# A hybrid decoder layer on one core: the order of instructions and the places of tiles drawn again, with activation functions of one table kept together

## The chip, the cores and the metric

The kernel runs on one core of a Trainium2 chip. The metric is the device time of one execution in microseconds. The kernel before was timed in three runs: 811.6, 809.67 and 811.94 us, with a median of 811.6 us.

## What is computed

One layer of a decoder over 512 tokens of width 1024, in float32: three token mixers side by side, each with a gate, then a projection, and a SwiGLU feed-forward network, with RMS norms ahead of and behind both.

```python
u = rms_norm(h, ln_mix_pre[l])
proj = jnp.einsum('bsd,de->bse', u, w_in[l])
qa, ka, va, qb, kb, vb, qm, gl = jnp.split(proj, split_idx, axis=-1)
y_swa = swa_sink_attention(...)          # window 128, 8 query heads
y_sb = stick_breaking_attention(...)     # 8 heads, log_sigmoid and exp
y_mem = memory_cross_attention(...)      # 4 heads, softmax over 256 memory rows
g = jax.nn.sigmoid(gl.reshape(B, S, N_BRANCH, D))
merged = g[:, :, 0] * (y_swa @ w_swa) + g[:, :, 1] * (y_sb @ w_sb) + g[:, :, 2] * (y_mem @ w_mem)
mix = jnp.einsum('bse,ed->bsd', merged, w_out[l])
h = h + rms_norm(mix, ln_mix_post[l])
u = rms_norm(h, ln_ffn_pre[l])
a = jax.nn.silu(jnp.einsum('bsd,df->bsf', u, w_gate[l])) * jnp.einsum('bsd,df->bsf', u, w_up[l])
ffn = jnp.einsum('bsf,fd->bsd', a, w_down[l])
h = h + rms_norm(ffn, ln_ffn_post[l])
```

So ScalarE needs sigmoid for the gates and the stick-breaking heads, Exp for both softmaxes, Ln and Exp for every inverse root of a norm, and silu's table set in the FFN.

## The kernel before

Every fp32 product is done as three matmuls: a tile is split into a high part (`hi`, a cast on ScalarE) and a remainder (`lo`, a subtraction on VectorE), and hi·hi, hi·lo and lo·hi are added up in PSUM (`mm3`). The big projections and the FFN are cut into two by two blocks, with seven products in place of eight. Sums of weight blocks come out of DMAs that add while they load (`raw` and `wide` tiles), others from VectorE.

The stages are: the first norm and projections (to about 80 us), the stick-breaking heads (80 to 205), the sliding-window heads in four pairs (`swa_pair`, from 205), gates and branch projections, the memory attention in two pairs (`mem_pair`, 318 to 363, tiles `mw`, `mpts`), the memory gates and the sum of the three branches (`merge`, tiles `mg`), the mixing (about 420 to 480), the FFN (480 to 793) and the last norm.

In the mixing, `mix(t)` does one block t of 128 tokens. Eight times three matmuls for each half fill two PSUM banks. ScalarE squares both with a sum (`mt<-p`), `rstd_small` makes the inverse root from the sums with a Ln and an Exp on ScalarE and four small steps on VectorE (tiles `s`), VectorE scales the bank (`mt<-p,s,bc_g_post`), and adds it to the residual (`xr`). A second square, a second Ln and Exp, and a scaling (`mt<-xr,s,bc_g_fpre`) make the FFN's input, which TensorE transposes (`turn(t)`, `p<-c_ident,mt`). ScalarE casts it out of PSUM into the FFN's right-hand sides (`B11h`, `B21h`, `T1h` and so on). The first gate of the FFN is a sigmoid `sg` and a product `aq` on VectorE. At the end `dn_half` does the same kind of norm for the output: `sqr`, Ln, Exp, and `fg`.

PSUM has eight banks, `p0` to `p7`. `raw`, `hi`, `lo` have four places each, small tiles (`s`) sixteen and tiles of 128x512 (`ck`) 73. Class `Places` hands them out: the n-th tile of a kind goes to the place that the table `PLAN` gives.

The order on each engine is fixed. `tile_kernel` first issues all instructions, stage by stage, and class `Noted` writes down each (its inner function is line 186, which is why the profile has this line for all). The last loop adds, for each engine, a chain of order-only dependencies by the table `ORDER`, whose ranges are indices of the recorded instructions. `table(name)` records an explicit load of a set of activation functions; there are nine of these. The build then puts another table load ahead of any activation whose function isn't in the set that is loaded at that point of ScalarE's list.

The lines in question:

```python
nc.scalar.activation(tmp[h][:, :], ps[h][:, :], AF.Square, accum_out=ss[:, h : h + 1])
fn(t, s1, AF.Ln, bias=b, scale=1.0 / D)          # rstd_small
fn(r, t, AF.Exp, scale=-0.5)
table("natural_log_exp_and_others")               # ahead of mix_mm(0, 0, KC)
table("silu_and_others")                          # behind mix(3)
for part in text.split():                         # text is a row of ORDER
    a, _, b = part.partition("-")
    for k in range(int(a), int(b or a) + 1):
        if last is not None:
            follow(seen[k], seen[last])
        last = k
```

Of the kernel before, what the change touches and what calls it, by code (L numbers as in the profile page):

```python
# [100 lines left out]
    ),  # L101
    "gpsimd": (
        "5-8 4 9-12 2-3 0-1 13-14 16 15 17 31-32 18-19 24 29 20-23 25-28 30 33-36 38-39 41 37 42 40 43-50 52 51 54 53 "
        "55-59 61 60 62-66 69 67 72 68 70-71 73-79 81 80 82-89 91 90 92-117 129-132 118-119 133 120-121 134 122-128"
# [1952 lines left out]
```

## Time and profile before

| | us |
|---|---|
| median of three runs | 811.6 (809.67 to 811.94) |
| profiled execution | 809.63, span 807.9 |
| granted TensorE clock, mean | 0.991 |
| idle time of TensorE, start to 80 us | 2.29 |
| DMA from HBM | 125.70 MB, 161 GB/s over the span |

The page's slices show where TensorE is not full, in tenths of each fortieth of the span (20.2 us):

```profile
PE   8999999999999999989998979999999999999994
ACT  7663778976966675798947896445454547758765
PEclk9999999999999999999999999999999999999998
DMA  8543864534599888898998017986777755879302
```

A 9 is 90% or more. TensorE (PE) falls to 8 or 7 in four slices ahead of the last: those that begin at 0, 343, 424 and 465. ScalarE (ACT) is never full for long. The table loads are instructions of ScalarE, named ACT_TABLE_LOAD, and no line of the program's own but of the helper.

### The profile page before, as it was taken

To read this page: it belongs to the slowest core of one execution; us is meant where nothing else is said; L and a number is where in the kernel's file an instruction comes from. 1 tells how busy PE (TensorE), PEld (TensorE's weight loads), DVE (VectorE), ACT (ScalarE), POOL (GpSimd) and SP (SyncE) were. 2 spreads that over 40 slices of the span, in tenths; PEclk is the share of its full clock that TensorE was granted. 3 is DMA by queue.
4 is the path that set the end of the run, shared out by engine and by line. 5 is a ranking of instruction groups with operands and counts; after the bars stand their busy time and mean duration, and the time that the engine had idled before them with its cause. 6 is when DMAs were issued, how large, how long until landed. Compare 5 with 4: busy or idle time off the path is not lost.

```text
span 807.9 us, 12635 instructions
## 1 busy us (share of the span) xinstructions
PE 776.7 (96%) x4686; PEld 680.9 (84%) x4686; DVE 618.3 (77%) x997; ACT 547.2 (68%) x926; POOL 110.0 (14%) x139
## 2 busy tenths in 40 slices
PE   8999999999999999989998979999999999999994
PEld 6899898778689887778786779999999999888883
DVE  7995786678786856878976479877777778998865
ACT  7663778976966675798947896445454547758765
POOL 3110300110112112311021000100000000215000
PEclk9999999999999999999999999999999999999998
DMA  8543864534599888898998017986777755879302
GB/s 289 172 111 117 295 186 132 130 75 107 93 233 183 188 190 182 204 270 193 247 284 157 0 32 188 269 224 179 183 184 187 179 153 184 163 182 198 57 0 104
DMA packets 47565, 135.43 MB, mean 168 GB/s; under 512 B 5520, under 2 KB 7104, under 8 KB 47504
## 3 DMA queue, kind: packets, MB, share of 16 engines
q0 software_dynamic: 16640, 50.61, 34.2%
q1 hardware_dynamic: 30432, 83.63, 31.7%
q8 instruction: 36, 0.59, 0.3%
q10 hardware_dynamic: 432, 0.39, 0.2%
q14 instruction: 25, 0.20, 0.1%
HBM read 125.70 MB, written 4.72 MB: 161 GB/s over the span
## 4 chain that ended last, share of the span: by engine, by line
PE 42%; ACT 6%; DVE 2%; issue 1%; DVEq 0%; ACTq 0%
PE p L186 42%; ACT L186 3%; ACT mt L186 1%; DVE mt L186 1%; ACT s L186 1%; DVE s L186 0%; ACT hi L186 0%; DVE fg L186 0%; DVE xr L186 0%; DVE mg011l L186 0%; ACT sqr L186 0%; DVEq L2045 0%; ACT B11h L186 0%; ACT mg011h L186 0%; ACT mg001h L186 0%
## 5 line engine op out<-in xcount | busy, mean ns | idle before, releaser
L186 DVE TENSOR_TENSOR lo<-raw,hi 128x1024 fp32r<-128x1024 f32 (+5 forms) x118 | 134.0, 1138 | 41.4 <-ACT hi L186 40.6
L186 ACT CAST hi<-raw 128x1024 fp32r<-128x1024 f32 (+5 forms) x118 | 116.2, 986 | 71.8 <-PE p L186 56.4
L186 ACT CAST hi<-wide 128x1024 fp32r<-128x1024 f32 x83 | 87.2, 1052 | 83.9 <-PE p L186 50.2
L186 DVE TENSOR_TENSOR lo<-wide,hi 128x1024 fp32r<-128x1024 f32 x83 | 101.4, 1223 | 39.9 <-ACT hi L186 39.6
L186 ACT ACT_TABLE_LOAD x47 | 60.3, 1283 | 7.0 <-DVE s L186 4.1
L186 PE MATMUL p<-hi,uh 128*128 128x512 f32 (+1 forms) x160 | 58.1, 363 | 2.4 <-ACT mw L186 2.4
L186 PE MATMUL p<-lo,lh 128*128 128x512 f32 x154 | 59.9, 389 | 0.0
L186 PE MATMUL p<-hi,lh 128*128 128x512 f32 x154 | 59.9, 389 | 0.0
L186 PE MATMUL p<-hi,ll 128*128 128x512 f32 x154 | 59.9, 389 | 0.0
L186 PE MATMUL p<-lo,uh 128*128 128x512 f32 (+1 forms) x160 | 57.4, 359 | 0.0
L186 PE MATMUL p<-hi,ul 128*128 128x512 f32 (+1 forms) x160 | 57.2, 358 | 0.0
L186 PE MATMUL p<-uh,hi 128*128 128x512 f32 (+1 forms) x136 | 50.9, 375 | 1.4 <-ACT uh L186 0.9
L186 PE MATMUL p<-uh,lo 128*128 128x512 f32 (+1 forms) x136 | 49.6, 365 | 0.0
L186 PE MATMUL p<-ul,hi 128*128 128x512 f32 (+1 forms) x136 | 49.6, 366 | 0.0
L186 PEld LDWEIGHTS p<-hi,uh 128*128 128x128 f32 x160 | 30.2, 189 | 6.6 <-ACT mw L186 3.1
L186 POOL DMA_DIRECT2D raw<-in_w_gu x17 | 14.6, 861 | 148.5 <-DMA raw<-in_w_gu 148.1
L186 PEld LDWEIGHTS p<-hi,lh 128*128 128x128 f32 x154 | 28.9, 188 | 6.0
L186 PEld LDWEIGHTS p<-hi,ll 128*128 128x128 f32 x154 | 28.9, 188 | 6.0
L186 PEld LDWEIGHTS p<-lo,lh 128*128 128x128 f32 x154 | 28.9, 188 | 5.9
L186 PEld LDWEIGHTS p<-hi,ul 128*128 128x128 f32 x160 | 30.1, 188 | 3.8
L186 PEld LDWEIGHTS p<-lo,uh 128*128 128x128 f32 x160 | 30.2, 189 | 3.4
L186 DVE TENSOR_TENSOR_SCAN bw<-br,bw 128x512 f32<-128x512 f32 (+3 forms) x32 | 23.9, 804 | 10.3 <-ACT bw L186 10.3
(878 smaller groups left out, 2490.1 us busy)
## 6 DMA issues: line engine op xcount, KB each, us to landing
wide<-in_w_gu SPq DMA_DIRECT2D x31, 512.0 KB, 4.8
raw<-in_w_gu SPq DMA_DIRECT2D x26, 512.0 KB, 4.7
raw<-in_w_g POOLq DMA_DIRECT2D x18, 512.0 KB, 5.6
raw<-in_w_gu POOLq DMA_DIRECT2D x17, 512.0 KB, 7.1
raw<-in_w_g SPq DMA_DIRECT2D x14, 512.0 KB, 4.7
raw<-in_w_p SPq DMA_DIRECT2D x11, 512.0 KB, 4.9
bp<-in_w_dn SPq DMA_DIRECT2D x22, 256.0 KB, 4.4
wide<-in_w_gu POOLq DMA_DIRECT2D x10, 512.0 KB, 5.9
```

The costliest lines, as they stand in the source:

```text
L186: ins = f(*args, **kw)
```

## The change

The tables `ORDER` and `PLAN` are replaced by others; no code outside them differs. In `ORDER` the rows of TensorE, VectorE, ScalarE, GpSimd and SyncE are others; in `PLAN` the places of `lo`, `p`, `ck`, `s`, `fraw` and `flo`. Two rows of ScalarE's table, before and now:

```diff
-        "358 354 359 369 356 361-364 370 365-368 371-375 380 376-379 381 394 382-383 408 384-385 414-415 395-396 "
-        "418-419 386-389 397 390-393 402 398-399 409 403 410 400-401 411 424 404-405 425 406-407 412-413 433-434 416 "
+        "361-364 370-372 365-368 373-376 380 377-379 381 394-396 382-385 414-415 418-419 386-389 397 390-393 402 "
+        "398-399 408 403 400-401 409 404-405 410-411 406-407 412-413 424-425 416 433-434 440 417 441 432 449 420-421 "
```

Line numbers shift by two, so that the helper is line 188 in the changed kernel. The counts of all instructions are the same, except for ScalarE's table loads: 47 before and 9 now, the explicit ones. The numbers behind a name stand for its buffer.

ScalarE at the start of the memory attention's exponentials (`mw`), where `hi_76` is a cast of a branch weight. Before:

```order
L186 ACTIVATE gq0p_2992<-p_106,wide_84 128x512
L186 CAST hi_78<-raw_72 128x1024
L186 CAST hi_76<-wide_84 128x1024
L186 ACT_TABLE_LOAD
L186 ACTIVATE mw_3019,s_90<-p_110,s_93,wide_84 128x256 x2
L186 ACTIVATE mw_3020,s_90<-p_111,s_93,wide_84 128x256 x2
```

And now:

```order
L188 ACTIVATE gq0p_2992<-p_109,wide_84 128x512
L188 CAST hi_78<-raw_72 128x1024
L188 ACT_TABLE_LOAD
L188 CAST hi_76<-wide_84 128x1024
L188 ACTIVATE mw_3019,s_90<-p_110,s_88,wide_84 128x256 x2
L188 ACTIVATE mw_3020,s_90<-p_111,s_88,wide_84 128x256 x2
```

The table load has moved ahead of the cast `hi_76`; the exponentials stand behind both as before.

ScalarE in the mixing, with the end of block 0 and the squares, Ln and Exp of block 1: `mt_3999<-p` and `mt_4000<-p` are block 1's two squares, the small activations on `s` are Ln and Exp, first of block 0's second norm and then of block 1's first, and `mt_3999<-xr` is block 1's second square. Before:

```order
L186 ACTIVATE mt_3999,s_90<-p_106 128x512
L186 ACT_TABLE_LOAD
L186 ACTIVATE s_93<-s_91,s_92 128x1
L186 CAST hi_77<-wide_84 128x1024
L186 ACT_TABLE_LOAD
L186 ACTIVATE s_91<-s_93 128x1
L186 ACTIVATE mt_4000,s_90<-p_105 128x512
L186 ACT_TABLE_LOAD
L186 ACTIVATE s_91<-s_90,s_88 128x1
L186 ACT_TABLE_LOAD
L186 ACTIVATE s_89<-s_91 128x1
L186 ACTIVATE mt_3999,s_91<-xr_3814 128x512
```

And now:

```order
L188 ACTIVATE mt_3999,s_88<-p_107 128x512
L188 ACTIVATE s_89<-s_91,s_90 128x1
L188 CAST hi_77<-wide_84 128x1024
L188 ACTIVATE s_90<-s_89 128x1
L188 ACTIVATE mt_4000,s_88<-p_104 128x512
L188 ACTIVATE s_90<-s_88,s_93 128x1
L188 ACTIVATE s_92<-s_90 128x1
L188 ACTIVATE mt_3999,s_90<-xr_3814 128x512
```

The order of squares, cast, Ln and Exp is the same, and the four table loads between them are gone.

VectorE at the end of the mixing: `s` is the last step of block 3's inverse root, `mt_4186` and `mt_4187` are block 3's FFN input, which TensorE waits for, and `aq` the product of the first gate of the FFN. Before:

```order
L186 TENSOR_TENSOR lo_81<-raw_72,hi_76 128x1024
L186 SCALAR_TENSOR_TENSOR s_88<-s_93,s_88 128x1
L186 TENSOR_TENSOR aq_4309<-gp_4259,sg_4307 128x256
L186 SCALAR_TENSOR_TENSOR mt_4186<-xr_3822,s_88,bc_g_fpre_3832 128x512
L186 SCALAR_TENSOR_TENSOR mt_4187<-xr_3823,s_88,bc_g_fpre_3833 128x512
L186 TENSOR_TENSOR N2l_4382<-t_4269,N2h_4381 128x2x128
```

And now:

```order
L188 TENSOR_TENSOR lo_81<-raw_72,hi_76 128x1024
L188 SCALAR_TENSOR_TENSOR s_90<-s_88,s_90 128x1
L188 TENSOR_TENSOR N2l_4382<-t_4269,N2h_4381 128x2x128
L188 SCALAR_TENSOR_TENSOR mt_4186<-xr_3822,s_90,bc_g_fpre_3832 128x512
L188 SCALAR_TENSOR_TENSOR mt_4187<-xr_3823,s_90,bc_g_fpre_3833 128x512
L188 TENSOR_TENSOR aq_4309<-gp_4259,sg_4307 128x256
```

`aq` has moved behind the two `mt`, and the subtraction `N2l` ahead of them.

At the end of the kernel the last rows of ScalarE are the same but for eight table loads that are gone. On SyncE and GpSimd only the order among the FFN's weight loads (`raw<-in_w_gu` and `wide<-in_w_gu`) is another: 46 and 10 rows of difference.

More of the change, by code (lines that the diff above doesn't have):

```diff
@@ L120 @@
     "lo": (
-        "0 1 2 3 1 2 0 3 1 2 0 3 1 2 0 3 1 2 0 3 1 2 0 3 1 2 0 3 1 2 0 3 1 0 2 3 1 0 2 3 1 0 2 3 1 0 2 3 1 0 2 3 1 0 2 "
-        "3 1 0 2 3 1 0 2 3 1 0 2 3 1 0 2 3 1 0 2 3 1 0 2 3 1 0 2 3 1 0 2 3 1 0 2 3 1 0"
+        "0 1 2 3 1 2 0 3 1 2 0 3 1 2 0 3 1 2 0 3 1 2 0 3 1 2 0 3 1 2 0 3 1 2 0 3 1 2 0 3 1 2 0 3 1 2 0 3 1 2 0 3 1 2 0 "
+        "3 1 2 0 3 1 2 0 3 1 2 0 3 1 2 0 3 1 2 0 3 1 2 0 3 1 2 0 3 1 2 0 3 1 2 0 3 1 2"
     ),
     "p": (
[5 rows of a table removed]
[5 rows of a table added]
     ),
@@ L132 @@
         "1 3 4 6 13 15 18 8 10 12 16 17 19 21 23 22 24 25 27 26 29 28 30 14 3 31 32 4 14 14 4 33 34 35 3 31 32 36 37 31 "
[19 rows of a table removed]
[19 rows of a table added]
     ),
     "s": (
-        "0 3 2 1 0 2 0 3 1 2 0 1 0 3 2 1 0 2 0 3 1 2 5 4 5 2 4 5 5 2 4 5 5 3 4 2 3 4 4 1 5 3 2 3 0 5 3 1 1 5 0 1 2 1 3 "
-        "0 1 2 2 3 5 6 0 6 4 5 6 0 0 4 5 0 0 5 3 1 4 10 8 9 6 0 10 4 2 10 4 0 7 4 0 10"
+        "0 3 2 1 0 2 0 3 1 2 0 1 0 3 2 1 0 2 0 3 1 2 0 1 0 2 1 0 0 2 1 0 0 3 1 2 3 0 2 4 1 2 0 2 5 1 2 4 4 0 5 6 1 6 3 "
+        "5 6 1 1 3 0 4 5 4 2 0 4 2 2 5 0 2 2 0 3 1 5 10 8 9 4 2 10 5 6 10 5 2 7 5 2 10"
     ),
     "fraw": (
-        "4 5 0 1 3 2 7 8 6 4 5 0 1 3 4 2 6 1 0 8 4 7 5 3 2 1 8 6 0 4 5 2 3 7 1 6 4 8 0 5 3 1 7 2 6 8 5 4 0 3 7 6 2 1 8 "
-        "4 3 5 0 7 2 8 1"
+        "4 5 0 1 3 2 8 7 6 4 5 0 1 3 4 2 6 1 7 0 8 4 3 5 2 1 0 7 6 8 3 2 5 4 1 7 8 6 0 3 5 1 4 2 7 6 3 0 8 5 4 7 2 1 6 "
+        "0 5 8 3 4 2 6 1"
     ),
```

166 rows, old and new, of tables (ORDER, PLAN) are left out of this document.

## The prediction

> **What bounds the kernel now.** I first read the page's busy list and the page's list of the costliest groups, which say what there is to win:
>
> ```profile
> PE 776.7 (96%) x4686; PEld 680.9 (84%) x4686; DVE 618.3 (77%) x997; ACT 547.2 (68%) x926; POOL 110.0 (14%) x139
> L186 ACT ACT_TABLE_LOAD x47 | 60.3, 1283 | 7.0 <-DVE s L186 4.1
> ```
>
> TensorE is busy for 776.7 us of a span of 807.9, so 31.2 us is all that an order can give back, apart from matmuls that ran at a lower clock. ScalarE spends 60.3 us in 47 table loads of 1283 ns. ScalarE is busy for 68% only, so those 60.3 us are no gain in themselves. A load counts where TensorE, or the end of the kernel, waits for what stands behind it. So the next view is the busy time by stage. Its columns are the stretch, its length, the busy time of PE, PEld, DVE, ACT and POOL (with counts), the granted clock, the share of time that the DMA engines were busy, and GB/s.
>
> ```profile
> 205.00:225.00 20.00, 18.15 (x99) 13.95 (x98) 16.24 (x50) 19.21 (x46) 3.45 (x4) 1.00 0.57 99
> 318.00:331.00 13.00, 10.55 (x44) 8.00 (x43) 10.46 (x23) 10.42 (x24) 1.72 (x2) 0.87 0.70 177
> 331.00:348.00 17.00, 17.00 (x96) 14.73 (x95) 14.81 (x23) 12.93 (x20) 6.10 (x7) 1.00 0.99 220
> 348.00:363.00 15.00, 12.77 (x62) 9.79 (x61) 10.85 (x22) 14.94 (x32) 2.71 (x3) 1.00 1.01 272
> 432.00:449.00 17.00, 13.46 (x57) 10.66 (x55) 7.60 (x19) 12.43 (x23) 0.86 (x1) 0.90 0.55 114
> 449.00:467.00 18.00, 14.44 (x73) 11.38 (x71) 8.69 (x25) 14.88 (x31) 0.00 (x0) 1.00 0.00 0
> 467.00:480.00 13.00, 10.47 (x86) 10.29 (x87) 10.15 (x22) 11.54 (x22) 0.00 (x0) 1.00 0.06 8
> 480.00:793.00 313.00, 313.00 (x2213) 295.50 (x2214) 254.97 (x349) 187.38 (x290) 35.53 (x41) 1.00 0.66 166
> ```
>
> Length less PE's busy time is TensorE's idle time: 1.85 us in the sliding-window attention (205 to 225), 2.45 and 2.23 in the memory attention (318 to 331 and 348 to 363), and 3.54, 3.56 and 2.53 in the mixing (432 to 480), which is 9.63 there. In the FFN (480 to 793) it is zero, whatever ScalarE does. Behind 793 the kernel only finishes. TensorE's list of waits (what it waited for, us in all, times, the longest) names who held it up:
>
> ```profile
> PE p L186 <- DVE mt L186: 7.3, 4, 3.5
> PE p L186 <- ACT mw L186: 3.0, 3, 1.8
> PE p L186 <- ACT B11h L186: 2.3, 1, 2.3
> ```
>
> `mt` and `B11h` are tiles of the mixing, `mw` the weights of the memory attention. All of them are made on ScalarE, or on VectorE right behind ScalarE, just where the loads stand.
>
> **The change, part by part.** The instructions are the same on every engine, except that ScalarE's list has 9 table loads in place of 47. The FFN's weight loads, and many rows on the other engines, change places by a few rows.
>
> *The mixing.* For each block of 128 tokens two squares give sums, Ln and Exp give the inverse root, and VectorE's `mt` empties the PSUM bank that TensorE needs next. ScalarE, VectorE and TensorE show this for block 1:
>
> ```profile
> 435.90 1.28 ACT L186 ACT_TABLE_LOAD   x1 [1.40 <-DVE s L186]
> 437.19 0.29 ACT L186 ACTIVATE s<-s,s 128x1 f32<-128x1 f32 x1
> 437.51 1.28 ACT L186 ACT_TABLE_LOAD   x1
> 438.80 0.20 ACT L186 ACTIVATE s<-s 128x1 f32<-128x1 f32 x1
> 439.49 1.41 DVE L186 SCALAR_TENSOR_TENSOR mt<-p,s,bc_g_post 128x512 f32<-128x512 f32 x2
> 437.02 0.39 PE L186 MATMUL p<-wo07h,mg111l 128*128 128x512 f32 x1
> 440.95 0.50 PE L186 MATMUL p<-wo10h,mg001h 128*128 128x512 f32 x1 [3.54 <-DVE mt L186]
> 442.25 0.63 PE L186 MATMUL p<-wo11l,mg001h 128*128 128x512 f32 x1
> 442.68 0.63 PE L186 MATMUL p<-wo11h,mg001l 128*128 128x512 f32 x1
> 432.43 1.28 ACT L186 ACT_TABLE_LOAD   x1
> ```
>
> From 435.90 to the end of `mt` at 439.49 + 1.41 = 440.90 it is 5.00 us, 2 x 1.28 of it loads; 2.44 is left. The load at 432.43, and the one before its Ln, push back the chain of block 0 ahead of it, so the start moves 2.56 earlier as well, to 433.34, and the bank is free at 435.78. TensorE needs it when its last matmul before the wait (start 437.02) is through, 0.39 later at the latest, so the wait of 3.54 goes, with more than a us to spare. That is why block 1 pays for four loads but gives back no more than the wait. A second loss goes with it: right behind the wait matmuls start 442.68 - 442.25 = 0.43 apart, and the clock of this stretch is 0.90, that is at most 17 x 0.10 = 1.7 us lost; I take 1.5. Blocks 2 and 3 have the same chain. The last wait differs:
>
> ```profile
> 476.93 1.28 ACT L186 ACT_TABLE_LOAD   x1
> 479.91 0.63 PE L186 MATMUL p<-c_ident,mt 128*128 128x128 f32 x4 [2.53 <-DVE mt L186]
> ```
>
> On VectorE `mt` stands behind `aq`, the first gate of the FFN, which needs a sigmoid with its own load (476.93). The new order puts `mt` ahead of `aq`, and this load's place in the chain goes with the two of Ln and Exp: 3.84 against a wait of 2.53. What comes next is the cast `B11h` behind the copies and squares on ScalarE: I leave 0.5 us for it. **Term: 9.63 + 1.5 - 0.5 = 10.6.** From both sides: 11.3 if nothing is left (9.63 + 1.7), and 5.3, half, if casts and copies, which now run one behind the other, take the loads' place.
>
> *The end.* Five rows of the chain that ended last, with a row of ScalarE and one of TensorE at the same time:
>
> ```profile
> 793.93 1.28 ACT L186
> 797.52 1.41 DVE fg L186 x2
> 799.01 1.28 ACT L186
> 800.62 1.28 ACT L186
> 802.15 0.23 DVE s L186
> 796.95 0.58 ACT L186 ACTIVATE sqr<-p 128x512 f32<-128x512 f32 x1
> 796.17 0.39 PE L186 MATMUL p<-hi,ll 128*128 128x512 f32 x1
> ```
>
> From 793.93 to 800.62 four loads stand on this chain, 5.13 us. The first two hold back block 2's last `fg`, and behind that VectorE starts block 3's sums. The other two lie between block 3's sums and its last scale at 802.15. Without them block 2 is out of the way, and block 3 waits for TensorE alone, whose last matmul ends at 796.17 + 0.39 = 796.56. Behind it come the square with its sum (0.7), VectorE's sum (0.1), Ln 0.29, Exp 0.20, by the rows of block 1 above, and VectorE's product with the gain, which was done beside a load and now is 0.7 in the path less what Ln and Exp cover: 1.5 in all, so 798.05 for what starts at 802.15. **Term: 4.1**, between 2.6 (the last two loads alone) and 5.1 (all four).
>
> *The memory attention.*
>
> ```profile
> 320.93 1.05 ACT L186 CAST hi<-wide 128x1024 fp32r<-128x1024 f32 x1 [1.72 <-DMA wide<-in_w_brt]
> 322.00 1.28 ACT L186 ACT_TABLE_LOAD   x1
> 324.55 0.50 PE L186 MATMUL p<-hi,uh 128*128 128x512 f32 x1 [1.78 <-ACT mw L186]
> 221.73 0.50 PE L186 MATMUL p<-hi,xsp60h 128*128 128x512 f32 x1 [1.49 <-ACT hi L186]
> 397.20 1.05 ACT L186 CAST hi<-wide 128x1024 fp32r<-128x1024 f32 x1 [1.08 <-DMA wide<-in_w_brt]
> ```
>
> At 318 to 331 the load for Exp stands behind a cast that waits 1.72 us for its transfer. Now it stands ahead of the cast and hides in this wait, so the exponentials `mw` come 1.3 us sooner, and the bank that they empty is taken up later. Of the idle 2.45, and of 13 x 0.13 = 1.7 lost to the clock (taken as 1.25), I leave 0.7: **3.0**, from 1.3 (the load alone) to 4.15. At 348 to 363 two loads and gate sums around the second pair's exponentials go: 2.6 us sooner against an idle time of 2.23: **2.2**, from 0 (if the transfers set this stretch, whose DMA share is 1.01) to 2.3.
>
> *The smaller ones.* At 205 to 225 two loads stood ahead of the cast for which TensorE waits 1.49 us; the idle time there is 1.85, of which I take **1.3** (0 to 1.85). The cast at 397.20 waits 1.08 us for a transfer, not for a load: **0**, from -1 to 1, since transfers move. In the FFN the loads of table sets, and two at its end, lie where TensorE never waits: **0**. The new order of weight loads in it costs nothing while casts run ahead of TensorE; what it costs otherwise is the last rival's price.
>
> **The sum** is 10.6 + 4.1 + 3.0 + 2.2 + 1.3 = 21.2 us. The profiled execution took 809.63 us (span 807.9 and 1.7 around it), so 788.4. The three runs have their median at 811.6, 2.0 above; the next median may lie as far above its profile, so up to 790.4. I take **788.5**, near the lower end, since every residue has been left out of the gain already.
>
> **Two rules weighed.** The rows above show a load ending at 435.90 + 1.28 = 437.18 and the Ln starting at 437.19. The Trainium skill, "ScalarE: Activation LUTs", section "What ACT_TABLE_LOAD costs", puts a drain of the pipeline on top of the load, about 2.7 us for a switch. By that the four loads of the end would hold 4 x 2.7 = 10.8, an estimate; the trace has no room for it, and the load alone is counted.
>
> The clock fell behind a wait of 3.54 (stretch of 0.90), and with a longest wait of 1.78 (stretch of 0.87), but not behind the wait of 2.53 (1.00). The Trainium skill, "TensorE: Matmul & The Clock Gate", section "Part 1: The HAM clock gate", lets the clock halve after an idle window of about 3.4 us. The first and the last agree, the second does not; by that page its 1.25 would stay out of the sum, which would give 789.8.
>
> **The rivals.**
>
> *Transfers take the place* of the wait. In 331 to 348 and 348 to 363 the DMA engines are busy 0.99 and 1.01 of the time, and two casts wait for transfers already (320.93 and 397.20). If TensorE gets there sooner and the weights don't, the memory attention's 3.0 + 2.2 comes back as a wait for DMA: 788.5 + 5.2 = 793.7. Against it: nothing in the mixing hangs on it, where the share is 0.55 and below. Chance 0.17.
>
> *Half of the mixing stays*, since the squares, copies and casts on ScalarE (12.43 and 14.88 busy in 17 and 18 us, loads in it) still come late: 788.5 + 5.3 = 793.8. Chance 0.14; both of these, 799, 0.04.
>
> *Everything goes*, the residues of 0.5, 0.7 and 0.55 and the cast's 1.08 at 397.20 too: 788.5 - 2.8 = 785.7, and with the upper bounds of the clock's two terms (0.2 and 0.45) and of the end (1.0) 784.0. Chance 0.12.
>
> *Slower: the FFN's casts wait.* The rows are ScalarE's waits in the FFN (480 to 793) and the page's issues (KB, us to landing):
>
> ```profile
> ACT hi L186 <- PE p L186: 66.8, 52, 2.8
> ACT hi L186 <- DVE wide L186: 24.3, 12, 2.5
> wide<-in_w_gu SPq DMA_DIRECT2D x31, 512.0 KB, 4.8
> ```
>
> Twelve casts wait already for sums `wide`, which need transfers; the others wait for TensorE, 66.8 / 52 = 1.28 us each, which is the least cover that a cast has. If the new queue order brings each of the twelve one transfer (4.8) later, it costs 4.8 - 1.28 = 3.5 each and 42 in all: 788.5 + 42 = 830. It decides from seven casts on (7 x 3.5 = 24.5). Against it: TensorE is busy 313.00 of 313. Chance 0.03.
>
> *The change doesn't do what it says*: loads come back, or their time was cover for something else in each place: 811.6. The list of ScalarE holds 9 loads, so 0.03.
>
> **How the numbers follow.** The forecast itself has 0.47. The range of 783 to 797 takes in the forecast, each of the two partial rivals and the case of all gone; outside are both partial ones together, no change, and slower, with some of the terms' own spread, in all under 0.2. A measurement of this kernel tells about 0.3%, 2.4 us, from no change. Faster by more: 0.47 + 0.17 + 0.14 + 0.04 + 0.12 = 0.94; within: 0.03; slower: 0.03.
>
> **What would show it.** TensorE's idle time from 432 to 480 falls from 9.63 to about 0.5 and no stretch there has a clock under 1. From the last matmul's end to the end of the span it takes 7.2 us in place of 11.3. The memory attention's first wait for `mw` is under 1 us. The FFN is as long as before, to 0.5 us. I am wrong if waits for transfers stand between 330 and 420, if `B11h` or another cast shows with more than 2 us in TensorE's list of waits, or if the FFN has idle time.

## The result, and the profile after

The changed kernel takes 789.5 us (median of four runs, 789.17 to 791.93) against 811.69 us before: a ratio of 0.9738, with a 95% interval of 0.9713 to 0.9763. The forecast was 788.5, in a range of 783 to 797. The time came out 1.0 us from it, but not all of its terms did: two errors of opposite sign lie under the sum.

The profiled execution of the changed kernel has a span of 788.9 us, 19.0 less than before. It is the longest of its four runs: the spans of the others are 786.6 to 786.9. The page's busy list, and the first four rows of TensorE's list of waits of this execution (what it waited for, us in all, times, the longest):

```profile
PE 772.8 (98%) x4686; PEld 681.5 (86%) x4686; DVE 617.7 (78%) x997; ACT 499.4 (63%) x888; POOL 109.8 (14%) x139
```
```profile
PE p L188 <- ACT mw L188: 5.0, 1, 5.0
PE p L188 <- DVE wide L188: 1.4, 1, 1.4
PE p L188 <- ACT uh L188: 1.1, 1, 1.1
PE p L188 <- ACT cq2p L188: 0.9, 1, 0.9
```

The waits for `mt` (7.3) and `B11h` (2.3) are gone altogether. A wait for `mw` of 5.0 us stands there that was not there before; the three waits for `mw` were 3.0 in all. The stages, in the columns of the table shown before (length, busy PE, PEld, DVE, ACT, POOL, granted clock, DMA share, GB/s):

```profile
205.00:225.00 20.00, 19.79 (x112) 15.32 (x110) 16.50 (x50) 17.52 (x43) 4.31 (x5) 1.00 0.62 108
316.00:331.00 15.00, 14.53 (x75) 11.74 (x74) 13.94 (x28) 13.71 (x30) 4.71 (x6) 1.00 0.84 189
331.00:345.00 14.00, 14.00 (x75) 12.06 (x74) 11.59 (x19) 7.34 (x12) 3.96 (x5) 1.00 1.08 259
345.00:360.00 15.00, 10.03 (x42) 7.98 (x41) 8.77 (x19) 11.87 (x26) 1.84 (x2) 0.77 0.89 218
392.00:400.00 8.00, 7.09 (x32) 5.53 (x31) 6.20 (x10) 5.67 (x10) 0.00 (x0) 1.00 0.98 248
415.00:480.00 65.00, 65.00 (x411) 58.78 (x410) 49.05 (x106) 39.27 (x98) 6.91 (x8) 1.00 0.50 110
480.00:775.00 295.00, 295.00 (x2075) 278.17 (x2075) 239.81 (x323) 170.59 (x263) 33.82 (x39) 1.00 0.67 168
```

TensorE is never idle in the mixing (415 to 480) and never in the FFN. In the memory attention's first part (316 to 331) 0.47 us are left of 2.45, and the clock is full. The second part (345 to 360) is worse than before: 4.97 us of idle time where there were 2.23 (348 to 363 then), and a clock of 0.77.

The chain that ended last shows where the rest of the gain lies. Before, it went from instruction to instruction through the mixing and the end; this is it after, from the last wait for a transfer on:

```profile
396.78 385.01 PE p L188 x2594
...
782.30 0.20 ACT sqr L188
782.51 0.02 issue
782.53 0.16 DVE s L188
...
783.21 0.22 DVE s L188
...
783.65 0.75 DVE fg L188
784.40 0.66 DVEq L2047
```

From 396.78 to the last matmul's end at 781.79 TensorE runs without a break, 385.0 us. Before, the same work went from 398.78 to 796.56, 397.8 us. So the mixing and the FFN gave 12.8 us. Up to that point TensorE is 2.0 us earlier (396.78 against 398.78). Behind the last matmul the span goes on for 788.9 - 781.8 = 7.1 us, against 11.3. That is 12.8 + 2.0 + 4.2 = 19.0, the whole difference of the two spans.

The new wait has this row on TensorE, and these on ScalarE (timeline) and in the chain that ended last:

```profile
350.48 0.69 PE L188 MATMUL p<-c_ident,mw 128*128 128x128 f32 x2 [4.97 <-ACT mw L188]
346.09 0.56 ACT L188 ACTIVATE mw<-p,s,wide 128x256 f32<-128x256 f32 x1 [5.78 <-DMA gq0p<-bs]
335.29 10.71 DMA gq0p<-bs
```

TensorE transposes the second pair's exponentials. ScalarE was idle for 5.78 us ahead of the first of them, and what ended the idle time is a transfer on GpSimd's queue that landed 10.71 us after its issue. `gq0p<-bs` adds a branch's sum `bs` to a gate. `mw` neither reads nor writes either of them. So the first thing to ask was why an exponential waits for it.

### The profile page after: what moved, and what is told of

Its sections match the earlier page's. It is cut to its first block, busy times and chain, and to the rows that moved or that the text cites. A ratio compares the mean times of both kernels' runs of the same rounds, so it can differ in the third digit from the quotient of the medians.

```text
span 788.9 us, 12610 instructions
## 1 busy us (share of the span) xinstructions
PE 772.8 (98%) x4686; PEld 681.5 (86%) x4686; DVE 617.7 (78%) x997; ACT 499.4 (63%) x888; POOL 109.8 (14%) x139
## 4 chain that ended last, share of the span: by engine, by line
PE 93%; DMA 3%; ACT 2%; issue 1%; DVE 1%; DVEq 0%; ACTq 0%; POOLq 0%
PE p L188 93%; DMA gq0p<-bs 1%; DMA wide<-in_w_brt 1%; ACT mw L188 1%; DMA raw<-in_w_p 0%; ACT hi L188 0%; DVE s L188 0%; ACT cq0p L188 0%; DVE lo L188 0%; DVE fg L188 0%; ACT gq0p L188 0%; DVEq L2047 0%; ACT uh L188 0%; ACT cq2p L188 0%; DVE pts L188 0%
## 5 line engine op out<-in xcount | busy, mean ns | idle before, releaser
L188 DVE TENSOR_TENSOR lo<-raw,hi 128x1024 fp32r<-128x1024 f32 (+5 forms) x122 | 139.0, 1142 | 45.5 <-ACT hi L188 44.8
L188 ACT CAST hi<-raw 128x1024 fp32r<-128x1024 f32 (+5 forms) x122 | 120.4, 989 | 85.0 <-PE p L188 69.2
L188 ACT CAST hi<-wide 128x1024 fp32r<-128x1024 f32 x79 | 82.9, 1052 | 73.9 <-PE p L188 56.4
L188 DVE TENSOR_TENSOR lo<-wide,hi 128x1024 fp32r<-128x1024 f32 x79 | 96.4, 1222 | 33.4 <-ACT hi L188 33.1
L188 POOL DMA_DIRECT2D raw<-in_w_gu x15 | 12.9, 861 | 136.9 <-DMA raw<-in_w_gu 136.5
L188 PEld LDWEIGHTS p<-uh,hi 128*128 128x128 f32 x136 | 25.6, 189 | 6.2 <-ACT uh L188 1.6
```

What stands on the lines that cost most here:

```text
L188: ins = f(*args, **kw)
```

## The experiments

All of the kernels below but the last are the one before or the changed one with a few indices of the tables moved, by these two functions, put behind the tables:

```python
def moved(engine, *pairs):          # index k of the recorded instructions goes right behind index j
    o = []
    for part in ORDER[engine].split():
        a, _, b = part.partition("-")
        o += range(int(a), int(b or a) + 1)
    for k, j in pairs:
        o.remove(k)
        o.insert(o.index(j) + 1, k)
    ORDER[engine] = " ".join(map(str, o))

def swapped(first, *pairs):         # from tile `first` on, two places of 128x512 tiles are exchanged
    o = PLAN["ck"].split()
    for a, b in pairs:
        to = {str(a): str(b), str(b): str(a)}
        o[first:] = [to.get(n, n) for n in o[first:]]
    PLAN["ck"] = " ".join(o)
```

In the kernel before, eight of the nine explicit table loads stand too early in ScalarE's order, by 5 to 35 rows. The load for Ln and Exp ahead of the mixing, for instance, stands 19 rows early, ahead of four more sigmoids. The build puts a load of another set in front of the first of these, and from there on each Ln and each Exp gets one of its own. Moving the explicit load behind the last sigmoid, and the next one, for silu, behind the last Exp, removes all of these, with no other instruction moved. That allows the loads to be taken out stage by stage, in the old order and at the old places.

### The loads at the end alone

```diff
+moved("scalar", (701, 699))
```

> The kernel before with one table load moved: the explicit load ahead of the last norm stands behind the last silu instead of ahead of it, so that the 8 loads between the last Ln and Exp activations go, and two more at the end of the FFN; nothing else differs. Theory (loads on the chain that ended last): faster by 4.1 us, between 3.6 and 4.6, so about 807.5, with the time from the last matmul's end to the end of the span 7.2 us in place of 11.3, and everything ahead of 790 us as before. Rival (a switch costs more than its row, 2.7 us each): faster by some 10. Rival (the loads were cover for TensorE's end or the output's transfer): within 1.3 us of before, half of the loads or less.

Measured: 807.46 us (805.94 to 808.98, eight runs) beside 811.52 for the kernel before, ratio 0.995, interval 0.9933 to 0.9967. That is 4.1 us. The last matmul ends at 798.97 and the span at 806.11, so 7.1 us behind it. The end gave what the theory said, and the loads did not cover anything. ScalarE's list has nine loads fewer, not ten. One point did not hold in the profiled execution: the time ahead of the last matmul was not as before, but 2.4 us longer (798.97 against 796.56). The instructions there are the same, but waits and clock are not the same from one execution to the next: the second wait of the mixing, for one, is 2.63 here and 0.98 in the kernel before.

### The loads in the mixing alone

```diff
+moved("scalar", (471, 455), (524, 515))
```

> The kernel before with two explicit table loads moved, behind the last gate's sigmoid and ahead of the first silu, so that the loads inside the mixing go; the order of everything else, and all places, as before. Theory (the loads are what TensorE waited for in the mixing): faster by 10.5 us, between 9 and 12, so about 801; the clock of 432 to 449 back at 1.00; what is left of TensorE's idle time in the mixing is at its end, 1 to 2.5 us, since on VectorE the product with the first silu still stands ahead of the last block's scaling and the silu keeps its load. Rival (squares, casts and copies, or the order on VectorE, take the place of half of the loads): faster by 5 to 6. Rival (the new order and places did it, not the loads): faster by less than 3.

Measured: 798.68 us (797.01 to 799.1), ratio 0.9839, interval 0.9815 to 0.9862: 12.8 us. The loads are what TensorE waited for, and the order and places of the changed kernel aren't needed for it. The expectation was too small, and one step of it was wrong: nothing is left at the end of the mixing. The stage of this kernel, and below it the same stretch of the kernel before:

```profile
415.00:480.00 65.00, 65.00 (x403) 58.44 (x402) 49.00 (x107) 38.03 (x97) 6.78 (x8) 1.00 0.51 113
```
```profile
415.00:480.00 65.00, 55.36 (x296) 46.65 (x295) 36.45 (x82) 50.95 (x95) 5.19 (x6) 0.97 0.42 86
```

TensorE does 403 matmuls in the stretch where it did 296. In this kernel `aq` still stands ahead of the last `mt` on VectorE, and the silu (`sg`, called a sigmoid further up) keeps one load, the explicit one. The chain ahead of it has become so much shorter that this costs nothing.

### All the loads, in the old order

```diff
+moved("scalar", (76, 75), (196, 173), (282, 273), (283, 282), (360, 359), (408, 393),
+      (471, 455), (524, 515), (701, 699))
```

Pair 283 moves a sigmoid behind the last exponential of the sliding-window heads; the other eight are table loads.

> The kernel before with all eight misplaced table loads moved, and one sigmoid with them, so that ScalarE's list holds 9 loads; the order of everything else, and all places, as before. Theory (the loads are nearly the whole change): faster by 17 to 21 us, so 791 to 795, close to the changed kernel's 789.5. Rival (the new order and places are worth as much as the loads): faster by 12 or less.

Measured: 788.05 us (786.95 to 788.55), ratio 0.971, interval 0.9687 to 0.9733. That is a gain of 23.5 us, more than expected, and as much as the whole change: its interval overlaps that of the changed kernel. So all that the change brought can be had from nine moves in ScalarE's order. The three stages alone make 12.8 + 4.1 + 2.6 = 19.5 (the last one is below). The other 4.0 belong to the three loads ahead of the memory attention, as far as the intervals allow to tell: TensorE's idle time at 80 to 100 and 205 to 225 falls from 2.33 to 0.44, and the rest was not traced. The new order and places bring nothing in sum. The next runs show that they bring some and cost some.

### The new wait: places

Each 128x512 tile has a place, and a tile can be written only when the last reader of the place's tile before it is through. By the tables, the changed kernel gives `mw20` the place of `bs30`, `mw21` that of `bs20` and `mw30` that of `bs31`. The transfers `gq0p<-bs` read these. That of `bs30` is the last in the queue. The kernel before gives `mw20` the place of `bs31`, whose transfer is two earlier. Two versions of the changed kernel move the exponentials to places that have long been read:

```diff
+swapped(342, (47, 9), (15, 13), (6, 20))      # y_places: mw20, mw21, mw30
+swapped(342, (47, 9))                         # y_one: mw20 alone
```

> The changed kernel with three pairs of places of 128x512 tiles exchanged from the second pair of the memory attention on: the exponentials mw20, mw21 and mw30 take the places of tiles that are long read, in place of those of bs30, bs20 and bs31, whose transfers on GpSimd's queue are under way (TensorE waits 4.97 us for mw there, and the transfer lands at 346.0). Theory (the exponentials wait for their place): the wait falls to 0.5 to 1.5 us, the clock behind it stays at 1.00, and the kernel is faster than the changed one by 4 to 5.5 us, so 784 to 785.5. Rival (bandwidth: the transfers set this stretch, and the next tile that is loaded comes late instead): the wait for mw goes, others for transfers come between 345 and 400, and the gain is under 1.5 us.

> The changed kernel with one exchange of places alone: the exponential mw20 leaves bs30's place, while mw21 keeps that of bs20, whose transfer lands about 1.6 us ahead of that of bs30, and mw30 that of bs31. Theory (each exponential waits for its own place): mw20 starts at about 340.5, mw21 right behind the landing of bs20 at 343 to 344.5, and TensorE's wait for mw falls from 4.97 to between 1 and 3 us, so a time between 784.5 and 787.5. Rival (the wait is for the queue of transfers as a whole, not for a place): the wait stays above 4 us, and the time within 1.2 us of 789.5.

Measured: three exchanges 783.58 us (782.97 to 785.34), ratio 0.966, interval 0.9637 to 0.9683. One exchange 783.4 us (783.08 to 783.87), ratio 0.9663, interval 0.9648 to 0.9678. Both are faster than the changed kernel beyond the intervals, by 6 us, which is more than was expected of either. The stages and ScalarE's timeline of the version with one exchange:

```profile
331.00:345.00 14.00, 14.00 (x75) 12.06 (x74) 12.61 (x23) 11.54 (x25) 4.00 (x5) 1.00 1.08 257
345.00:360.00 15.00, 15.00 (x76) 12.40 (x75) 14.28 (x25) 14.79 (x28) 3.44 (x4) 1.00 1.06 285
```
```profile
340.28 0.56 ACT L198 ACTIVATE mw<-p,s,wide 128x256 f32<-128x256 f32 x1
...
341.96 0.56 ACT L198 ACTIVATE mw<-p,s,wide 128x256 f32<-128x256 f32 x1 [0.48 <-DMA gq0p<-bs]
```

`mw20` starts at 340.28, right behind the casts ahead of it, in place of 346.09. `mw21` still waits for its own place, by 0.48 us, until the transfer of `bs20` has landed. This is the mechanism in one row: each exponential waits for the place that it is written to. The wait of TensorE is gone, and so is the low clock. The DMA share is 1.06 to 1.08 in this stretch, where the changed kernel had 1.08 and 0.89, and TensorE waits for no transfer: bandwidth wasn't the limit. The expected remainder of 1 to 3 us with one exchange didn't come. I had taken the landing of `bs20` at 343 or later from the changed kernel's trace; in this run it came at 341.9, and TensorE needs the tile only at 345.

### The memory attention alone, in the old order

```diff
+moved("scalar", (360, 359), (408, 393))
```

> The kernel before with two explicit table loads moved, so that the loads around the exponentials of the memory attention's first and second pair go (one stands ahead of the cast that waits for its transfer, one behind the last exponential); all else as before. Theory (the loads held the first pair, and the second pair waits for places whose transfers are under way): TensorE's lost time from 300 to 340 falls by 2.5 to 3.5 us, from 340 to 400 it stays within 1 us of before, and the kernel is faster by 1.5 to 3, so about 809.2. Prediction's own terms (both pairs gain): faster by 5.2. Rival (all comes back as waits for transfers): within 0.7 us of before.

Measured: 808.38 us (805.83 to 810.99, twelve runs) beside 811.01, ratio 0.9971, interval 0.9956 to 0.9986: 2.6 us. The halves of the stage, of this kernel and then of the kernel before:

```profile
300.00:340.00 40.00, 39.06 (x189) 32.12 (x188) 31.56 (x50) 28.45 (x50) 11.28 (x13) 1.00 0.83 192
340.00:400.00 60.00, 58.17 (x273) 46.69 (x272) 51.30 (x81) 53.88 (x93) 8.79 (x11) 1.00 0.96 242
```
```profile
300.00:340.00 40.00, 37.53 (x174) 30.44 (x174) 30.58 (x49) 27.85 (x48) 10.45 (x12) 0.96 0.79 177
340.00:400.00 60.00, 56.91 (x269) 45.94 (x268) 49.79 (x78) 54.12 (x90) 9.62 (x11) 1.00 0.97 236
```

In the first half the idle time falls from 2.47 to 0.94. The clock is at 1.00 too, which is up to another 40 x 0.04 = 1.6, but this can't be put down to the loads: in the runs with the mixing's and with the end's loads moved, the loads of this stage are in place, the idle time of the first half is 2.66 and 2.80, and the clock is 1.00 as well. In the second half the idle time falls by 1.3 only, a little more than the 1 us that the theory allowed. So the loads held the first pair, as the prediction had it; the second pair's loads were worth less than its 2.2.

### Both in the old order

```diff
+moved("scalar", ...)                                   # as in the run with all loads
+swapped(342, (54, 9), (69, 20), (62, 66), (15, 61))
```

> The kernel before with its eight misplaced table loads moved (788.05 us), and with four exchanges of places from the second pair of the memory attention on, so that mw20, mw21, mw30 and wo11h no longer stand in places of bs31, bs21, bs11 and bs20. Theory (places, in the old order too): the wo11h cast no longer waits for a transfer (it started at 343.39 on the landing at 343.37), TensorE's waits for mw (0.54 and 0.57) go, and the kernel takes 784.5 to 787. Rival (what limits there is something else, such as the copies that stand ahead of the exponentials in this order): within 1.2 us of 788.05.

Measured: 787.5 us (787.09 to 790.85), ratio 0.9721, interval 0.97 to 0.9741. Against 788.05 without the exchanges this is no difference that can be told, and the rival was right. ScalarE's timeline, with all loads moved, and then with the exchanges too:

```profile
343.39 0.62 ACT L199 CAST wo11h<-wo 128x512 fp32r<-128x512 f32 x1 [0.79 <-DMA gq0p<-bs]
343.92 0.56 ACT L199 ACTIVATE mw<-p,s,wide 128x256 f32<-128x256 f32 x1
```
```profile
340.08 0.59 ACT L207 COPY gq2p<-p 128x512 f32<-128x512 f32 x1
340.56 1.06 ACT L207 CAST hi<-wide 128x1024 fp32r<-128x1024 f32 x1
...
342.55 0.57 ACT L207 ACTIVATE mw<-p,s,wide 128x256 f32<-128x256 f32 x1
```

The wait for a place went, as meant. But in the old order a copy of a gate and a cast stand ahead of `mw`, so that it starts at 342.55 and not at 340.28, and TensorE's list still has waits for `mw`, of 0.7 and 0.6 us. With the new order one exchange gives 783.4. So the new order is worth about 4 us (787.5 against 783.4), and the new place of one tile costs about 6 (789.5 against 783.4). By TensorE's idle time some 2.7 of the 4 us lie between 316 and 400. Which of the moved rows bring them was not taken apart.

### The price of a load

```diff
+added("scalar", (819, 816), (820, 817))     # like moved(), but the two indices are new
+    for _ in range(2):
+        nc.scalar.preload_act_table_set("natural_log_exp_and_others")
```

> The changed kernel with two table loads of the set that is in place already, one ahead of the last Ln and one ahead of the last Exp, behind the last matmul. Theory (a load costs its row of 1.28 us on the path and nothing more): from the end of the last matmul to the end of the span 9.6 us in place of 7.13, between 9.2 and 9.8. Rival (a drain comes on top, 2.7 us a switch): 12.4 us.

Measured: 792.0 us in a single run; the last matmul ends at 779.52 and the span at 789.10, 9.58 us. The chain that ended last:

```profile
780.26 1.28 ACT L200
781.55 0.29 ACT s L200
781.87 1.28 ACT L200
783.15 0.22 ACTq L2061
```

Two loads cost 9.58 - 7.13 = 2.45 us, less than twice 1.28, since the first begins while VectorE makes a sum. There is nothing on top of a load. These two are of the set that is in place already; the loads of the kernel before lie between different sets (Ln's and Exp's), and there is nothing on top of them either: block 1's Ln ended at 437.19 + 0.29 = 437.48, and the next load began at 437.51 and ended at 438.79, 0.01 ahead of the Exp. This run also shows how far the wait for the place varies: the code there is that of the changed kernel, and TensorE waits 3.69 us for `mw`, not 4.97.

## Why the prediction was right, point by point

**The bound.** TensorE's idle time by stage, and its list of waits, named the right places. Nothing was gained in the FFN, where TensorE was full before.

**The mixing** was foreseen with 10.6 us, at most 11.3. It gave 12.8 by the spans, and 12.8 again with its loads moved alone. The mechanism was right and the size too small. The waits were 9.63 and the clock's loss at most 1.7, and the 0.5 us that was left as a rest did not stay. The other 1.5 us lie in matmuls that the busy time counts as work. The larger part is the last matmul ahead of each wait: the one at 437.02 counts as busy for 0.39 us, though the next one usually starts 0.23 behind. From 437.02 to 440.95 it is 3.93, so this wait cost 3.70, and not 3.54. Over the five waits from 437 to 480 that makes 0.8. A smaller part is a slow start: behind the wait of 3.54, matmuls began at 440.95 and 441.29, 0.34 apart. The rest, about half a microsecond, was not traced. The step that set `aq` behind `mt` was not needed, as the run with the mixing's loads alone shows.

**The end** was foreseen with 4.1 us: 4.2 by the spans, and 4.1 alone.

**The memory attention** is where a step failed. The first term, 3.0, came between the two profiled executions: in the changed kernel the lost time of this part is down to 0.47 us of idle time with the clock at 1.00. Its 1.25 for the clock was that one execution's, though, since two other runs with the same loads in place have 1.00 there. The second term was 2.2: "two loads and gate sums around the second pair's exponentials go: 2.6 us sooner against an idle time of 2.23". It turned into a loss of 2.7 us of idle time, and of the clock besides. The exponentials lost their loads but got places that a transfer still read. The prediction had the place changes in the text of the change and gave them no term at all. Its rival with the right result was "transfers take the place", which gave back 3.0 + 2.2. The result was right in the profiled execution, where both halves together gain nothing. The cause was another: not the time that the weights take, but the place of one tile. The prediction's own sign of being wrong, waits for transfers between 330 and 420, was there. One exchange of places brings the 6 us back, with a DMA share that is higher still.

**The smaller ones.** The sliding-window heads gave 1.85 - 0.21 = 1.6 for a term of 1.3. The first stretch (80 to 100), left out for its size, gave 0.5.

**The sum** of 21.2 was made against the profiled execution, and came out as 19.0 between the two spans, since the memory attention gave 5 us less than its terms and the other stages some 3 more. The medians differ by 22.2, because the profiled execution of the changed kernel was its slowest, by 2.1 us of span, and that of the kernel before one of its fastest (809.63, with a mean clock of 0.991, where other executions have 0.987 to 0.993). So it is in part luck that the forecast came within 1.0 us: 5 too much stood against 3 too little, and the median of the changed kernel lies 2.4 below its profiled execution (789.5 against 791.93). The run with two added loads, whose wait is 1.3 shorter than that of the profiled execution and whose clock falls less behind it, fits this: in the other runs of the changed kernel the wait is likely as short. That was not profiled.

**The rivals.** Half of the mixing left: refuted, TensorE is full there. The FFN's casts late: refuted, 295.00 busy of 295. This rival had no ground: the rows of GpSimd and SyncE in `ORDER` are the same in both kernels, and every weight load reads the same block in the same order. Only the places that some of them write to (`fraw`) differ, which the text on the change, and the prediction after it, took for another order. The change does nothing: refuted.

**The rules.** The load's price is its row, 1.28 us, in the last run as in the trace of the kernel before. The Trainium skill ("ScalarE: Activation LUTs", section "What ACT_TABLE_LOAD costs") adds a drain, to make 2.7 us of a switch to another set; the rows of the kernel before, whose loads are such switches, show none.

For the clock the prediction read the stretch of 467 to 480, but the wait of 2.53 ends with it. Its reading holds all the same: the clock behind that wait is 1.00, as the rows of the last section show.

## What to carry to other kernels

A table load costs only where the slowest engine waits behind it, so find those loads by the stage's idle time: the 38 loads that went here held ScalarE for 38 x 1.283 = 48.8 us, and cost 23.5. Explicit loads that stand a little too early can bring many automatic ones, 18 for two of them in the mixing: look at where each one stands against the last activation of the old set. When a planner draws order and places anew, read the places too: a tile that is written early must not get the place of one that a queued transfer still reads, and a wait that names a transfer whose data the instruction doesn't use is the sign of that.

## What was not expected of the hardware

The granted clock falls behind waits that are shorter than the one seen first, and not each time. With all of the mixing's loads in place, the wait of about 2.5 us at its end was followed by full clock in the kernel before, and by half the clock in the run with the end's loads moved, whose instructions up to there are the same. In all of the traces the low clock is 0.50, and behind the start-up and ahead of the last matmul's end it lasts 3.41 us, or twice that. Inside one execution its starts lie whole multiples of 3.41 apart (325.60 and 441.65 in the kernel before, 34 times). So the time can be cut into pieces of 3.41 us, counted from such a start. The end of the mixing in the kernel before, and then in the other run:

```profile
475.79:479.20 3.41, 1.58 (x14) 1.38 (x12) 1.95 (x5) 3.37 (x7) 0.00 (x0) 1.00 0.00 0
479.20:482.61 3.41, 2.70 (x24) 2.73 (x25) 3.41 (x6) 3.41 (x8) 0.45 (x1) 1.00 0.53 154
```
```profile
477.06:480.48 3.42, 1.36 (x12) 1.15 (x10) 2.18 (x5) 3.38 (x7) 0.00 (x0) 1.00 0.05 8
480.48:483.89 3.41, 2.93 (x14) 2.96 (x15) 2.44 (x5) 2.22 (x6) 0.56 (x1) 0.50 0.46 145
```

The second wait falls more into one piece, with TensorE busy for 1.36 us of it, and costs half the clock for the next piece, up to 1.7 us more for the same wait of 2.54. In the same run the wait of 3.54 in the mixing is split between two pieces, and costs no clock:

```profile
436.11:439.52 3.41, 1.56 (x7) 0.95 (x6) 0.26 (x2) 3.06 (x4) 0.00 (x0) 1.00 1.06 210
439.52:442.94 3.42, 1.73 (x8) 1.43 (x9) 2.92 (x7) 1.15 (x3) 0.00 (x0) 1.00 0.43 84
442.94:446.35 3.41, 3.41 (x17) 2.83 (x16) 0.16 (x1) 3.38 (x6) 0.00 (x0) 1.00 0.00 0
```

So what a wait costs in clock depends on how it lies to these pieces, and that differs from one execution to the next. In the ten traces the clock fell behind every full-clock piece with 1.36 us or less of busy TensorE, and behind none with 1.73 or more; between 1.56 and 1.67 both were seen, so the exact rule stays open. The Trainium skill ("TensorE: Matmul & The Clock Gate", section "Part 1: The HAM clock gate") gives an idle window of about 3.4 us. The length of the pieces agrees with it, but no idle time of that length is needed here: the wait of 2.54 is shorter. A wait of 4.97 us was followed by a stretch of 15 us at 0.77 (the changed kernel), one of 3.69 by 0.89 in the run with added loads.
